# A third buffer for each of the four tags of converted weights, and conversions up to three items ahead

## The chip, the cores and the metric

The kernel runs on one core of a Trainium2 chip. The metric is the device time of one execution in microseconds (us), lower is better; the kernel before is given by the median of three runs. Engines have the profile's names: PE is the matmul engine, PEld its weight loads, DVE the vector engine, ACT the scalar engine, POOL the GpSimd engine, SP the queue that issues most DMAs.

## The reference

One sequence of 512 tokens and width 1024 goes through three layers. The first has three branches (a state-space scan, a delta-rule scan, a gated linear scan), the other two have four (a gated recurrent branch and three kinds of attention). Every layer begins with one wide projection, merges its branches through gates, projects out, and ends with a gated feed-forward block of inner width 2816. Cut to the parts that the change touches:

```python
proj = jnp.einsum('bsd,de->bse', rms_norm(x, norm1_g), w_in)
...
x = x + merged.astype(dt) @ w_out
h2 = rms_norm(x, norm2_g)
ffn = (jax.nn.silu(h2 @ w_ffn_gate) * (h2 @ w_ffn_up)) @ w_ffn_down
return x + ffn
```

## The kernel before, in words

Activations lie feature-major, 128 features by 512 tokens a tile. Each float32 product is made of three float16 products: a weight is scaled by 64 and cut into a high and a low float16 part, as the activations are, and PE adds high x high, high x low and low x high in one PSUM bank (`fm_g`, L1181 to L1183: 128x512 products; `tm`, L1216 to L1218: 128x128 products, operands swapped).

**Weights come in items.** A plain item (a unit) is eight 128x128 blocks, 512 KB of float32. `_emit_unit` (L1057) issues its load on SP into a staging tile (`wst` or `bst`, two buffers each, L1060), converts the high part on ACT (L1070) into `whi` or `bhi`, and the low part on DVE (L1071) into `wlo` or `blo`. The foreground has the `w` tags, the background (the gate projections and the branch outputs) the `b` tags. One plain item of the foreground feeds 24 matmuls of `fm_g`.

**The feed-forward blocks** have a second sort of item. Every third block of the gate and up weights (7 of 22), and the whole down projection, are computed by a seven-product scheme on 256-token halves: `_emit_seventh` (L1092) makes one of the seven weight sums on DVE (L1106, L1110) from staged quarters, converts it on ACT (L1119) and DVE (L1120) into one tile that holds high and low, and puts it into whichever of the four tags is used least (L1115). A seventh with four blocks feeds 12 matmuls of 128x256 (`seventh`, L1424 to L1426). In the gate and up stage, two plain items come first, then a group of seven sevenths, then four plain items, and so on (the list `FOREGROUND`); the down stage is 84 sevenths.

**Who comes when.** `take` (L1136) is called when the matmuls of an item are about to be written. It first gives back the tags of the item before (L1144), then emits loads and conversions of coming items as long as `_room` (L1123) says so, then returns the item. `_room` counts buffers: the background may be one item past the present one (L1130); a plain foreground item needs fewer than three plain items from the present one to it, and fewer than two live buffers in `whi` and in `wlo` (L1133); a seventh needs one tag with fewer than two live buffers, in the feed-forward part only (L1134). A scheduler then orders the instructions of each engine: among those that are ready in its own model of the run, the one written first goes first. On the chip each engine's order is fixed, and an instruction that must wait holds up those behind it. A conversion therefore stands in ACT's and DVE's fixed order among other work: in the gate and up stage among the epilogue of a block (L1440 multiplies PSUM by the row norm on DVE, or on POOL for one of the two halves; L1478 is a tanh on ACT; L1480 on DVE; L1231 and L1235 cut the result into `hh` and `hl`; L1370 makes sums for the seven-product scheme).

After the feed-forward block of one layer the next projection's items follow in the same list, and the first plain ones are converted while the down stage still runs.

Of the kernel before, what the change touches and what calls it, by code (L numbers as in the profile page):

```python
# [11 lines left out]
F16 = mybir.dt.float16  # L12
# [13 lines left out]
PS = 1024.0  # L26
EPS = 1e-6
UB = 8
H = T // 2
FF7 = tuple(range(1, NF, 3))  # L30


def blocks(*ws):
# [6 lines left out]
    b = np.concatenate(seq) if len(seq) > 1 else seq[0]  # L40
    return np.ascontiguousarray(b.reshape(-1, UB, 128, 128).transpose(0, 2, 1, 3))


def paired(a, b):

    k, n = a.shape
    s = np.stack([w.reshape(k // 128, 128, n // 128, 128).transpose(2, 0, 1, 3) for w in (a, b)], axis=1)
    s = s.reshape(-1, UB, 128, 128)
    return np.ascontiguousarray(s.transpose(0, 2, 1, 3))
# [185 lines left out]
class First:  # L235
# [546 lines left out]
    def hgrn(self, yd):  # L782
# [19 lines left out]
        for h in range(4):  # L802
# [23 lines left out]
            nc.gpsimd.tensor_tensor(out=kk, in0=k2[:, 0], in1=k2[:, 1], op=ALU.add)  # L826
            pd = self.b("H")
            for i in range(4):
# [12 lines left out]
            for l in range(7):  # L841
# [6 lines left out]
                if l < 5:  # L848
                    po = self.b("H")
                    for i in range(4):  # L850
# [5 lines left out]
                else:  # L856
                    if l == 5:
                        big = self.b("H")
                    bv = big.rearrange("p (i t) -> p i t", i=4)
# [10 lines left out]
            for d in range(2):  # L870
# [5 lines left out]
                nc.gpsimd.tensor_tensor(out=qp, in0=q, in1=p, op=ALU.mult)  # L876
                pt = self.b("H")
                for i in range(4):
                    nc.tensor.transpose(pt[:, 128 * i:128 * i + 128], kr[:, 128 * i:128 * i + 128], self.ident)
                kt = self.hw()  # L880
                nc.scalar.copy(out=kt, in_=pt)
                pk = self.b("H")
                order = (0, 1, 2) if d == 0 else (3, 2, 1)
# [15 lines left out]
                yield  # L899
            po = self.b("H")  # L900
            for i in range(4):
# [62 lines left out]
class Net(First):  # L964
# [92 lines left out]
    def _emit_unit(self, s, name, u):  # L1057
        nc = self.nc
        tag = "wb"[s]
        st = self.t(self.wst, [128, UB, 128], tag + "st", F32, 2)  # L1060
        nc.sync.dma_start(out=st, in_=self.io[name][u])
        hi = self.t(self.wsp, [128, UB, 128], tag + "hi", F16, 2)
        lo = self.t(self.wsp, [128, UB, 128], tag + "lo", F16, 2)
        if s and self.spare and self.emitted[1] % 2:
            nc.scalar.activation(out=st, in_=st, func=AF.Copy, scale=WS)
            nc.scalar.copy(out=hi, in_=st)
            nc.gpsimd.tensor_tensor(out=lo, in0=st, in1=hi, op=ALU.subtract)
        else:
            for h in (slice(0, UB // 2), slice(UB // 2, UB)) if s and self.spare else (slice(0, UB),):
                nc.scalar.activation(out=hi[:, h], in_=st[:, h], func=AF.Copy, scale=WS)  # L1070
                nc.vector.scalar_tensor_tensor(out=lo[:, h], in0=st[:, h], scalar=WS, in1=hi[:, h], op0=ALU.mult, op1=ALU.subtract)  # L1071
        return hi, lo
# [19 lines left out]
    def _emit_seventh(self, e, name, u, m):  # L1092

        nc = self.nc
        if m == 0:
            st = self._stage(name, u)
            nxt = self.items[0][e + 7] if e + 7 < len(self.items[0]) else ("", 0, None)
            if nxt[2] is not None:
                self._stage(*nxt[:2])
        a11, a21, a22, a12 = self._stage(name, u)  # L1100
        n = a11.shape[1]
        if m in (0, 4, 6):
            src = {0: a11, 4: a22, 6: a12}[m]
        elif m == 5:
            src = self.s2
            nc.vector.tensor_tensor(out=src, in0=a12, in1=src, op=ALU.subtract)  # L1106
        else:
            src = self.t(self.tmp, [128, 4, 128], "bw", F32, 2)[:, 0:n]
            x, y = {1: (a21, a22), 2: (self.s2, a11), 3: (a11, a21)}[m]
            nc.vector.tensor_tensor(out=src, in0=x, in1=y, op=ALU.add if m == 1 else ALU.subtract)  # L1110
            if m < 3:
                self.s2 = src
        if m == 6:
            del self.staged[name, u]
        tag = min(("bhi", "blo", "whi", "wlo"), key=lambda t: self.tags[t])  # L1115
        o = self.t(self.wsp, [128, 2, 4, 128], tag, F16, 2)
        self.tags[tag] += 1
        hi, lo = o[:, 0, 0:n], o[:, 1, 0:n]
        nc.scalar.activation(out=hi, in_=src, func=AF.Copy, scale=WS)  # L1119
        nc.vector.scalar_tensor_tensor(out=lo, in0=src, scalar=WS, in1=hi, op0=ALU.mult, op1=ALU.subtract)  # L1120
        return hi, lo, tag

    def _room(self, s, e, i):  # L1123

        name, _, m = self.items[s][e]
        if e == i:
            return True
        if s:
            at = lambda n: n[-1] if n[:2] == "wi" or n[:3] == "wup" else "f"
            return e < i + 2 and at(name) == at(self.items[s][i][0])  # L1130
        if m is None:
            plain = sum(k is None for _, _, k in self.items[s][i:e + 1])
            return plain < 3 and all(self.tags[t] < 2 for t in ("whi", "wlo"))  # L1133
        return self.opened and min(self.tags.values()) < 2  # L1134

    def take(self, name, u, m=None):  # L1136
        s = int(self.bgmode)
# [1025 lines left out]
```

## Time and profile before

| what | value |
| --- | --- |
| median of three runs | 3617.13 us (3607.03 to 3620.99) |
| the profiled execution | 3613.31 us |
| its span, first to last instruction | 3611.6 us |
| mean granted TensorE clock | 0.976 |
| busy: PE, PEld, DVE, ACT, POOL | 92%, 56%, 76%, 45%, 21% |
| stages of gate and up weights in the span | 1056.7 to 1293.7, 2152.4 to 2396.1, 3251.1 to 3492.6 us |
| stages of down weights in the span | 1293.7 to 1402.7, 2396.1 to 2501.3, 3492.6 to the end |

A matmul's shown length includes its way through the array, and the next one starts before it ends; so the distance between two starts tells what a matmul takes of PE, and an idle time shown on PE is shorter than the time that PE lost. A row of the waits has the waiting engine and line, what it waited for, the total in us, the number of waits and the longest.

### The profile page before, as it was taken

The numbers are of one execution on the slowest core, as the hardware profiler recorded it, in microseconds if no ns is written. First come the engines' busy times: TensorE is split into PE (matmuls) and PEld (weight loads), VectorE is DVE, ScalarE is ACT, GpSimd is POOL, SyncE is SP. The second block draws the span as 40 slices with busy tenths as digits, with TensorE's granted clock in tenths as the row PEclk, the third lists the DMA queues.
The fourth block names the chain that finished last, engine by engine and source line by source line (L and its number), as shares of the span: only waits on it lengthen the run. The fifth ranks groups of instructions, "written<-read, shape, count | busy, mean of one in ns | idle before, by whom it ended". The sixth has DMA issues, their size and how long they took to land. (4 is left out here: it accounts for less than half of the span.)

```text
span 3611.6 us, 60781 instructions
## 1 busy us (share of the span) xinstructions
PE 3338.2 (92%) x23758; PEld 2033.9 (56%) x23758; DVE 2760.1 (76%) x5599; ACT 1608.3 (45%) x3009; POOL 752.6 (21%) x782
## 2 busy tenths in 40 slices
PE   7899999899899999999989999999999989999998
PEld 3565566555455577556545545568655545545567
DVE  6877777587777798788767677788788767777788
ACT  4232333255344344464556543344364455534443
POOL 2222223223332211201221132211201120132211
PEclk9999999899899999999999999999999999999999
DMA  4312213233242234323223353335322323363333
GB/s 141 82 57 59 75 49 91 72 126 114 88 164 94 94 106 146 106 63 96 93 82 109 116 159 96 96 112 159 111 65 80 94 90 100 112 185 110 94 100 94
DMA packets 151156, 368.16 MB, mean 102 GB/s; under 512 B 44098, under 2 KB 47428, under 8 KB 150868
## 3 DMA queue, kind: packets, MB, share of 16 engines
q1 hardware_dynamic: 117492, 336.03, 30.0%
q0 software_dynamic: 7680, 23.00, 1.9%
q10 hardware_dynamic: 25696, 5.25, 0.8%
q8 instruction: 186, 3.05, 0.4%
q14 instruction: 102, 0.84, 0.1%
HBM read 322.72 MB, written 40.04 MB: 100 GB/s over the span
## 5 line engine op out<-in xcount | busy, mean ns | idle before, releaser
L1181 PE MATMUL acc<-xh,whi 128*128 128x512 f16 x1224 | 469.5, 384 | 28.3 <-DVE g L1706 7.5
L1183 PE MATMUL acc<-xh,wlo 128*128 128x512 f16 x1224 | 469.0, 383 | 23.7 <-DVE wlo L1071 23.6
L1182 PE MATMUL acc<-xl,whi 128*128 128x512 f16 x1224 | 468.9, 383 | 0.0
L1070 ACT ACTIVATE whi<-wst 128x1024 f16<-128x1024 f32 x264 | 275.3, 1049 | 310.3 <-PE acc L1182 147.1
L1071 DVE SCALAR_TENSOR_TENSOR wlo<-wst,whi 128x1024 f16<-128x1024 f32 x264 | 353.9, 1341 | 15.9 <-ACT whi L1070 14.3
L1183 PEld LDWEIGHTS <-wlo 128*128 128x128 f16 x1824 | 179.6, 98 | 257.3 <-DVE wlo L1071 51.4
L1182 PEld LDWEIGHTS <-whi 128*128 128x128 f16 x1824 | 179.9, 99 | 226.6 <-issue 41.9
L1181 PEld LDWEIGHTS <-whi 128*128 128x128 f16 x1824 | 180.6, 99 | 210.4 <-issue 12.4
L1183 PE MATMUL bg<-xh,blo 128*128 128x512 f16 x596 | 230.9, 387 | 3.4 <-DVE reset L309 3.2
L1181 PE MATMUL bg<-xh,bhi 128*128 128x512 f16 x596 | 230.9, 387 | 0.4 <-DVE hk L810 0.4
L1182 PE MATMUL bg<-xl,bhi 128*128 128x512 f16 x596 | 230.6, 387 | 0.0
L1440 POOL TENSOR_TENSOR w<-w,w 128x512 f32<-128x512 f32 x66 | 117.5, 1780 | 448.4 <-DVE w L1440 282.1
L1216 PE MATMUL acc<-whi,xh 128*128 128x128 f16 x1152 | 195.1, 219 | 3.1 <-DVE xp L1758 1.3
L1218 PE MATMUL acc<-whi,xl 128*128 128x128 f16 x1152 | 195.0, 219 | 0.0
L1217 PE MATMUL acc<-wlo,xh 128*128 128x128 f16 x1152 | 195.0, 219 | 0.0
L1070 ACT ACTIVATE bhi<-bst 128x1024 f16<-128x1024 f32 (+1 forms) x132 | 121.7, 934 | 129.4 <-PE bg L1182 89.7
L1071 DVE SCALAR_TENSOR_TENSOR blo<-bst,bhi 128x1024 f16<-128x1024 f32 (+1 forms) x132 | 160.8, 1223 | 13.7 <-ACT bhi L1070 12.1
L1183 PE MATMUL bg<-xh,wlo 128*128 128x512 f16 x408 | 157.3, 386 | 9.1 <-DVE wlo L1071 9.1
L1181 PE MATMUL bg<-xh,whi 128*128 128x512 f16 x408 | 157.4, 386 | 3.0 <-ACT whi L1070 1.8
L1182 PEld LDWEIGHTS <-bhi 128*128 128x128 f16 x980 | 97.6, 100 | 109.0 <-issue 20.1
L1183 PEld LDWEIGHTS <-blo 128*128 128x128 f16 x980 | 97.5, 100 | 106.9 <-issue 6.8
L1181 PEld LDWEIGHTS <-bhi 128*128 128x128 f16 x980 | 97.9, 100 | 105.4 <-issue 9.8
(666 smaller groups left out, 9256.9 us busy)
## 6 DMA issues: line engine op xcount, KB each, us to landing
wst<-win SPq DMA_DIRECT2D x92, 512.0 KB, 3.6
bst<-win SPq DMA_DIRECT2D x64, 512.0 KB, 3.7
wst<-wff SPq DMA_DIRECT2D x60, 512.0 KB, 3.5
wst<-w SPq DMA_DIRECT2D x58, 512.0 KB, 3.6
gd<-bw SPq DMA_DIRECT2D x88, 256.0 KB, 2.2
ug<-gd SPq DMA_DIRECT2D x88, 256.0 KB, 2.7
wst<-wf SPq DMA_DIRECT2D x30, 512.0 KB, 3.5
bst<-w SPq DMA_DIRECT2D x20, 512.0 KB, 3.6
```

Of the source, the lines that this page charges most:

```text
L1070: nc.scalar.activation(out=hi[:, h], in_=st[:, h], func=AF.Copy, scale=WS)
L1071: nc.vector.scalar_tensor_tensor(out=lo[:, h], in0=st[:, h], scalar=WS, in1=hi[:, h], op0=ALU.mult, op1=ALU.subtract)
L1181: mm(ps, lhsT=wh, rhs=h[:, k, :], start=(k == 0), stop=False)
L1182: mm(ps, lhsT=wh, rhs=l[:, k, :], start=False, stop=False)
L1183: mm(ps, lhsT=wl, rhs=h[:, k, :], start=False, stop=(k == nk - 1))
L1216: mm(o, lhsT=xh, rhs=wh, start=(k == 0), stop=False)
L1217: mm(o, lhsT=xh, rhs=wl, start=False, stop=False)
L1218: mm(o, lhsT=xl, rhs=wh, start=False, stop=(k == 7))
L1440: tt = lambda eng, o, x, y, op=ALU.add: eng.tensor_tensor(out=o, in0=x, in1=y, op=op)
```

## The change

A constant `WB = 3` takes the place of the number 2 in the buffers of the four tags and in the rule of `_room`. Each tag has three tiles of 2 KB a partition instead of two, 8 KB a partition more in all. A plain foreground item may be emitted with up to three plain items from the present one to it, a background item up to two past the present one, and a seventh while any tag has fewer than three live buffers. The staging tiles stay at two buffers each. No instruction is added or taken out.

```diff
+WB = 3
...
-        hi = self.t(self.wsp, [128, UB, 128], tag + "hi", F16, 2)
-        lo = self.t(self.wsp, [128, UB, 128], tag + "lo", F16, 2)
+        hi = self.t(self.wsp, [128, UB, 128], tag + "hi", F16, WB)
+        lo = self.t(self.wsp, [128, UB, 128], tag + "lo", F16, WB)
...
-        o = self.t(self.wsp, [128, 2, 4, 128], tag, F16, 2)
+        o = self.t(self.wsp, [128, 2, 4, 128], tag, F16, WB)
...
-            return e < i + 2 and at(name) == at(self.items[s][i][0])
+            return e < i + WB and at(name) == at(self.items[s][i][0])
         if m is None:
             plain = sum(k is None for _, _, k in self.items[s][i:e + 1])
-            return plain < 3 and all(self.tags[t] < 2 for t in ("whi", "wlo"))
-        return self.opened and min(self.tags.values()) < 2
+            return plain <= WB and all(self.tags[t] < WB for t in ("whi", "wlo"))
+        return self.opened and min(self.tags.values()) < WB
```

## Rows read from the trace of the kernel before

**Rows 1.** The page's first part: busy time and share of each engine.

```profile
PE 3338.2 (92%) x23758; PEld 2033.9 (56%) x23758; DVE 2760.1 (76%) x5599; ACT 1608.3 (45%) x3009; POOL 752.6 (21%) x782
```

**Rows 2.** Busy time by stretch, the gate and up stages: stretch, us, engines, clock, DMA.

```profile
1056.70:1293.70 237.00, 224.38 (x1327) 128.45 (x1327) 186.20 (x307) 97.84 (x147) 48.11 (x30) 1.00 0.31 100
2152.40:2396.10 243.70, 225.11 (x1326) 127.66 (x1326) 185.90 (x306) 97.79 (x147) 48.09 (x30) 1.00 0.32 95
3251.10:3492.60 241.50, 226.53 (x1327) 128.41 (x1327) 186.17 (x307) 97.83 (x147) 48.08 (x30) 0.99 0.33 100
sum 722.20, PE 676.03 PEld 384.52 DVE 558.26 ACT 293.46 POOL 144.28; mean PE 225.34 PEld 128.18 DVE 186.09 ACT 97.82 POOL 48.09
```

**Rows 3.** PE's timeline: a stall, then 24 products of sevenths, then 48 of plain items.

```profile
2251.47 0.39 PE L1181 MATMUL acc<-xh,whi 128*128 128x512 f16 x1 [0.68 <-ACT whi L1070]
...
2252.91 0.39 PE L1183 MATMUL acc<-xh,wlo 128*128 128x512 f16 x1 [0.84 <-DVE wlo L1071]
...
2264.16 0.27 PE L1424 MATMUL bg<-xsh,blo 128*128 128x256 f16 x1
...
2266.78 0.27 PE L1424 MATMUL acc<-xsh,wlo 128*128 128x256 f16 x1
...
2278.89 0.38 PE L1181 MATMUL bg<-xh,whi 128*128 128x512 f16 x1
...
2289.25 0.38 PE L1181 MATMUL acc<-xh,whi 128*128 128x512 f16 x1
```

**Rows 4.** PE's waits for conversions in the whole span, longest in total first.

```profile
PE acc L1183 <- DVE wlo L1071: 23.6, 26, 1.9
...
PE bg L1183 <- DVE wlo L1071: 9.1, 7, 1.8
...
PE acc L1426 <- DVE whi L1120: 8.2, 12, 1.4
...
PE bg L1426 <- DVE whi L1120: 8.0, 9, 1.1
```

**Rows 5.** Busy time by stretch, the first two down stages, columns as above.

```profile
1293.70:1402.70 109.00, 102.41 (x926) 89.56 (x925) 103.55 (x176) 58.24 (x105) 17.39 (x11) 1.00 0.38 111
2396.10:2501.30 105.20, 102.09 (x925) 89.59 (x924) 98.81 (x176) 54.77 (x100) 12.10 (x12) 1.00 0.49 151
```

**Rows 6.** ACT's timeline around that stall: start, length, work, idle before it.

```profile
2237.82 1.99 ACT L1070 ACTIVATE whi<-wst 128x1024 f16<-128x1024 f32 x2
...
2247.68 0.63 ACT L1231 ACTIVATE hh<-w 128x512 f16<-128x512 f32 x1 [2.17 <-POOL w L1440]
2249.41 1.06 ACT L1231 ACTIVATE hh<-tt 128x1024 f16<-128x1024 f32 x1 [1.10 <-DVE tt L1370]
2250.37 1.04 ACT L1070 ACTIVATE whi<-wst 128x1024 f16<-128x1024 f32 x1
...
2270.92 1.99 ACT L1070 ACTIVATE whi<-wst 128x1024 f16<-128x1024 f32 x2
```

**Rows 7.** The costliest groups and the DMA issues: one conversion, one load.

```profile
L1070 ACT ACTIVATE whi<-wst 128x1024 f16<-128x1024 f32 x264 | 275.3, 1049 | 310.3 <-PE acc L1182 147.1
L1071 DVE SCALAR_TENSOR_TENSOR wlo<-wst,whi 128x1024 f16<-128x1024 f32 x264 | 353.9, 1341 | 15.9 <-ACT whi L1070 14.3
...
wst<-wff SPq DMA_DIRECT2D x60, 512.0 KB, 3.5
```

**Rows 8.** Waits of PE for the attention's own work, and of ACT for buffers.

```profile
PE O L1818 <- ACT pth L1231: 9.1, 9, 1.8
...
PE S L1581 <- ACT w L1572: 8.2, 7, 1.5
...
ACT whi L1070 <- PE acc L1182: 147.1, 53, 12.6
```

**Rows 9.** SP's timeline: loads of the two plain items after that group of sevenths.

```profile
2255.22 7.11 SPq L1061 DMA_DIRECT2D wst<-wff x2
```

**Rows 10.** Busy time by stretch, the second layer up to its feed-forward part, columns as above.

```profile
1402.70:2152.40 749.70, 705.41 (x5282) 404.78 (x5280) 562.28 (x1225) 376.87 (x746) 135.93 (x185) 0.99 0.35 107
```

## The prediction, made before the change was run

> **What bounds the kernel now.** I read the page's first part first: PE is busy for 92% of the span, DVE for 76%, ACT for 45% [rows 1]. PE is the engine to fill, so the question is where it stands still and for whom. The table by stretch answers by stage. In the three stages of gate and up weights DVE is busy 186 of some 240 us and ACT 98, so neither is full; yet PE is idle for 722.2 - 676.0 = 46.2 us in them [rows 2]. The timeline shows how a matmul should go there: 48 products of plain items start from 2278.89 to 2289.25, 0.216 us each, and 24 products of sevenths from 2264.16 to 2266.78, 0.109 us each [rows 3]. A stage has 30 plain items of 24 products and some 607 products of 256 columns or smaller (1327 less 720), so PE needs 720 x 0.216 + 607 x 0.109 = 221.7 us and takes 237.0, 243.7 and 241.5 [rows 2]: 57 us are lost in the three. The list of PE's waits then names the cause: its largest conversion rows, 23.6, 9.1, 8.2 and 8.0 us, hold 54 waits and 48.9 us, none over 1.9 us [rows 4]. They are about as large as the idle time of these stages and of the first two down stages together (46.2, and 6.6 + 3.1 [rows 5]). So conversions arrive late almost only in the feed-forward blocks, and nothing else stops PE in the gate and up stages.
>
> Why are they late, with ACT half idle? The episode at 2250 shows it. Two conversions run at 2237.8; the next stands in ACT's fixed order behind two splits of `hh`, which wait for POOL (2247.68) and for DVE (2249.41), and starts at 2250.37 [rows 6]. PE gets its high part at 2251.47 and its low part at 2252.91, with 0.68 and 0.84 us idle shown [rows 3]. By the rule of `_room` that conversion was for the item that PE was to start at once: after a group of sevenths just one plain item is ready beyond the one at work, because two buffers hold the item in use and the next.
>
> **The change, part by part.** *Buffers and rule for plain items.* I went through `take` by hand for a run of the list. Before, the item after the next is emitted only when PE's present item begins, and in the gate and up stage the lead is one plain item at every plain item. After, it is two; and the first two plain items behind a group of sevenths are emitted before or at that group's first product, where before the first of them came with the group's sixth. One plain item is 24 x 0.216 = 5.2 us of PE. A conversion is 1.05 us of ACT and 1.34 us of DVE [rows 7], unchanged in number and length. The longest shown lateness is 1.9 us [rows 4], under the 5.2 us of lead that is added, so all these stalls can go. The floor of the gain is the idle time shown, 46.2 us; the ceiling is the loss by the distance of starts, 57. An idle time is shown short by the part of a matmul that overlaps the next, 0.38 - 0.22 = 0.16 us [rows 3]; with some 45 of the waits in these stages that adds 7 and makes 53. I keep off 3 us for the norm's small sums, with which each stage begins and which stay (an allowance of mine), and take **50**, between the ends.
>
> *Rule for sevenths.* Twelve tiles instead of eight can be ahead. In the first two down stages PE is idle 6.6 and 3.1 us [rows 5], in the third its idle time is mixed with the kernel's end and I count nothing. DVE is busy 103.6 of 109.0 and 98.8 of 105.2 us there, so a deeper queue cannot feed PE for long; but it is filled in the stage before, where DVE has 50 us free, and four more tiles are a start. Ends 0 and 9.7; I take half, **5**. The Trainium skill (Perfetto Trace Analysis, section Identifying the Most-Contended Engine) holds VectorE's busy share to be a fair measure of how near a stage is to its limit; by that rule the down stages belong to DVE at 94 to 95%, buffers bring nothing there, this term is 0 and the forecast would come out 5 us higher.
>
> *Background, three items in flight instead of two.* Its conversions hardly hold PE today, so nothing is gained directly. Ends: see the next part.
>
> *Order in the other stages.* 264 foreground conversions [rows 7] less 90 of the gate and up stages are 174 that move one item ahead, in each case ACT's, DVE's and SP's instruction. Behind a waiting one on ACT stand the exponentials and splits of the attention, and PE waits for those: 9.1 and 8.2 us today [rows 8]. These could go, or double: ends -17.3 and +17.3. I take 0: the total work is the same, and a conversion still waits for a buffer that is freed at the same product as before. On SP a load moves ahead with it; it is hidden as long as two staging tiles suffice (first rival). The 8 KB a partition cost no time by themselves.
>
> *Sum.* 50 + 5 = 55 us off the profiled execution's 3613.3 (span 3611.6 and 1.7 around it): 3558. That execution is 3.8 us under the median of 3617.1, from which the same sum gives 3562; I say **3560**.
>
> **The rivals.** *Staging takes over.* The loads keep two staging tiles, and a group of sevenths holds one for long, so a conversion may wait for its load instead of its buffer. A plain item through one tile takes 3.5 us of load, 1.05 and 1.34 [rows 7], 5.9 us against 5.2 of PE: 0.7 late, and with two such items for each of 21 groups 30 us of the gain are lost: **3590**. Against it: the load of the item behind the sevenths was issued at 2255.22 [rows 9], so it should have landed near 2258.7, and its conversion ran at 2270.92 [rows 6]. Its tile lay full for 12 us because no buffer was free; staging is ahead of the conversions, not behind.
>
> *Conversions get in the way of the attention: slower.* ACT spends 147.1 us in 53 waits at conversions until PE frees a buffer, 2.8 us each [rows 8], and all that stands behind waits too. If the earlier place puts conversions in front of exponentials, splits and the scans' copies more often, each of the 174 costs PE a little. The gain is used up from 55 / 174 = 0.32 us each; at 0.45 us it is 78 us and the kernel ends at **3638**, slower. For it: PE is idle 44.3 of 749.7 us in the second layer up to its feed-forward part [rows 10], all of it with no conversion to blame, so it hangs on that chain. Against it: today's two largest waits of this kind are 17.3 us in all, and the rival needs more than four times that.
>
> *It does not do what it says.* Sevenths go into any tag, so they may take the third buffer of `whi`, on which plain items hang, and the scheduler may leave the conversions behind the same splits as now. Then the 1 or 2 us of lateness stay, and only the down stages gain: **3611**. Against it: by the walk through `take` plain items have both tags free for a lead of two in every group.
>
> **How the numbers follow.** About half a percent, 18 us, is what a measurement of this kernel can tell from no change: faster is under 3599, slower over 3635. The forecast has 0.67, staging 0.11 (still faster), no effect 0.09 (same), the attention rival 0.13, of which 0.09 slower and 0.04 in between. So faster 0.78, same 0.13, slower 0.09. The range begins where every lost us of the feed-forward blocks and the 17.3 come back, 3613 - 57 - 10 - 17 = 3529, and ends at staging with 17 us lost in the attention, 3607; that leaves out the attention rival and half of the case without effect, 0.17.
>
> **What would show it.** Right: PE's waits for `wlo` at L1183 and for `whi` at L1426 (one line lower in the new file) fall from 49 us to under 10; the three gate and up stages take 224 to 227 us each, with PE's idle time near 2; DVE's busy time there is still 186; the down stages shorten by 1 to 3 us. Staging would show as ACT and DVE waiting for `wst` and PE's waits for conversions of the items behind the sevenths remaining. The attention rival would show as stages from one feed-forward block to the next longer than 749.7, with more waits of PE for exponentials and splits. The forecast is wrong if the gate and up stages stay over 232 us, or if any attention layer moves by more than 10.

## The result, and the profile after

| what | before | after |
| --- | --- | --- |
| median of four runs, us | 3612.26 (3607.03 to 3620.99) | 3578.19 (3561.63 to 3583.99) |
| ratio, 95% interval | | 0.9896 [0.9855, 0.9936] |
| the profiled execution, us (span) | 3613.31 (3611.6) | 3583.99 (3582.3) |
| mean granted clock of it | 0.976 | 0.970 |

The kernel became 1% faster: 34 us by the medians, 29.3 by the two spans. (The ratios in this text are those on record, with their intervals; they differ a little from the ratio of the medians, here 0.9906.) The forecast was 3560; it is missed by 18 us and the result lies in its range. The profiled execution of after is the longest of its four. In the new file the lines of `Gen` touched here stand one lower (L1070 is L1071, L1183 is L1184, L1426 is L1427).

The page's first part, as [rows 1]:

```profile
PE 3345.5 (93%) x23758; PEld 2057.1 (57%) x23758; DVE 2740.0 (76%) x5599; ACT 1607.2 (45%) x3009; POOL 780.4 (22%) x782
```

Busy time by stretch, the three gate and up stages of after, columns and ends as in [rows 2]:

```profile
1073.80:1298.90 225.10, 223.34 (x1326) 130.13 (x1326) 179.39 (x305) 96.28 (x147) 55.03 (x30) 0.99 0.34 111
2161.60:2386.50 224.90, 221.88 (x1326) 129.76 (x1326) 179.13 (x302) 95.57 (x145) 55.04 (x30) 1.00 0.34 102
3238.50:3463.60 225.10, 223.16 (x1326) 130.15 (x1327) 178.90 (x302) 96.11 (x146) 55.04 (x30) 0.99 0.34 104
sum 675.10, PE 668.38 PEld 390.04 DVE 537.42 ACT 287.96 POOL 165.12; mean PE 222.79 PEld 130.01 DVE 179.14 ACT 95.99 POOL 55.04
```

The three stages take 675.1 us where [rows 2] have 722.2, and PE is idle 675.10 - 668.38 = 6.7 us in them where it was 46.2. PE's waits, all the rows for conversions in the span (total us, times, longest), show why:

```profile
PE acc L1427 <- DVE bhi L1121: 4.5, 4, 1.7
...
PE acc L1425 <- ACT bhi L1120: 1.7, 3, 0.9
...
PE acc L1427 <- DVE whi L1121: 1.0, 1, 1.0
...
PE bg L1184 <- DVE blo L1072: 0.7, 1, 0.7
...
PE acc L1427 <- DVE blo L1121: 0.5, 1, 0.5
```

The largest row of [rows 4], 23.6 us of plain products waiting for `wlo`, is gone altogether; 8.4 us are left of all kinds. Now the other stretches: first the two down stages that [rows 5] show, then the three stretches that lead up to a feed-forward block (the second of them is that of [rows 10]), all of after:

```profile
1298.90:1408.20 109.30, 102.72 (x925) 89.92 (x924) 106.07 (x178) 57.86 (x105) 19.09 (x11) 1.00 0.38 110
2386.50:2492.10 105.60, 101.81 (x925) 90.17 (x924) 101.02 (x179) 55.40 (x101) 14.93 (x12) 1.00 0.51 152
...
0.00:1073.80 1073.80, 962.55 (x6455) 584.32 (x6456) 774.59 (x1713) 402.28 (x784) 299.13 (x291) 0.93 0.29 90
1408.20:2161.60 753.40, 704.52 (x5282) 405.84 (x5281) 562.07 (x1225) 377.29 (x748) 133.79 (x185) 0.98 0.35 107
2492.10:3238.50 746.40, 699.78 (x5259) 402.94 (x5257) 554.78 (x1209) 376.75 (x747) 133.81 (x185) 0.99 0.35 108
```

and the same three stretches of before:

```profile
0.00:1056.70 1056.70, 944.21 (x6454) 570.81 (x6455) 777.49 (x1713) 400.06 (x782) 298.13 (x291) 0.95 0.30 92
...
2501.30:3251.10 749.80, 702.18 (x5258) 401.09 (x5257) 556.58 (x1208) 374.92 (x745) 133.40 (x185) 0.98 0.35 107
```

So the 29.3 us of the spans add up like this: gate and up stages -47.1; down stages +0.3, +0.4 and, with the kernel's end, -0.3 (119.0 to 118.7); second layer +3.7, third -3.4; first layer **+17.1**. The gain is there in full, and the first layer gives a third of it back. What it gives back is not a wait: PE is *busy* 962.55 us there instead of 944.21, 18.3 more for the same products, at a granted clock of 0.93 instead of 0.95. That clock is a mean over two levels, 1.2 and 2.4 GHz. One such stretch of after stands out, again by stretch:

```profile
682.00:691.60 9.60, 7.19 (x51) 4.84 (x49) 4.08 (x11) 3.04 (x7) 2.97 (x2) 1.00 0.09 17
691.60:718.90 27.30, 12.96 (x133) 10.21 (x134) 10.06 (x41) 3.38 (x13) 6.54 (x10) 0.50 0.36 119
718.90:728.00 9.10, 8.75 (x43) 4.01 (x41) 7.60 (x23) 1.37 (x2) 0.00 (x0) 1.00 0.26 93
```

For 27.3 us PE has half its speed; in the 9.6 us before it stood still for a quarter of the time, and it goes on standing still for half of it. It shows what low clock looks like, not where the 17 us went: e5 (below), whose whole first layer takes 1050.8 us, has as long a one at much the same work, and before has two there of 13.6 us each.

```profile
668.20:695.50 27.30, 13.65 (x138) 11.04 (x139) 10.12 (x39) 4.21 (x14) 6.43 (x10) 0.50 0.40 132
```

### The profile page after: what moved, and what is told of

It is laid out like the page before. It is cut to its first block, busy times and chain, and to the rows that moved or that the text cites. A ratio compares the mean times of both kernels' runs of the same rounds, so it can differ in the third digit from the quotient of the medians.

```text
span 3582.3 us, 60816 instructions
## 1 busy us (share of the span) xinstructions
PE 3345.5 (93%) x23758; PEld 2057.1 (57%) x23758; DVE 2740.0 (76%) x5599; ACT 1607.2 (45%) x3009; POOL 780.4 (22%) x782
## 4 chain that ended last, share of the span: by engine, by line
PE 36%; DVE 29%; issue 8%; ACT 6%; POOL 5%; DMA 3%; ACTq 0%; POOLq 0%; DVEq 0%; SPq 0%
PE bg L1182 3%; PE bg L1184 3%; PE bg L1183 3%; PE acc L1182 3%; PE acc L1183 3%; PE acc L1184 3%; DVE wlo L1072 3%; POOL w L1441 2%; DVE w L1441 2%; DVE bw L1111 2%; PE acc L1217 1%; PE acc L1218 1%; PE acc L1219 1%; PE acc L1425 1%; DVE hl L1236 1%
## 5 line engine op out<-in xcount | busy, mean ns | idle before, releaser
L1183 PE MATMUL acc<-xl,whi 128*128 128x512 f16 x1224 | 470.8, 385 | 0.0
L1184 PE MATMUL acc<-xh,wlo 128*128 128x512 f16 x1224 | 470.2, 384 | 0.0
L1071 ACT ACTIVATE whi<-wst 128x1024 f16<-128x1024 f32 x264 | 276.7, 1051 | 333.7 <-PE acc L1183 149.6
L1072 DVE SCALAR_TENSOR_TENSOR wlo<-wst,whi 128x1024 f16<-128x1024 f32 x264 | 330.3, 1252 | 29.7 <-ACT whi L1071 28.8
L1183 PEld LDWEIGHTS <-whi 128*128 128x128 f16 x1824 | 180.0, 99 | 241.8 <-issue 56.1
L1184 PEld LDWEIGHTS <-wlo 128*128 128x128 f16 x1824 | 180.0, 99 | 209.0 <-issue 13.7
L1184 PE MATMUL bg<-xh,blo 128*128 128x512 f16 x596 | 230.0, 386 | 3.2 <-DVE reset L310 3.2
L1183 PE MATMUL bg<-xl,bhi 128*128 128x512 f16 x596 | 230.3, 386 | 0.0
L1071 ACT ACTIVATE bhi<-bst 128x1024 f16<-128x1024 f32 (+1 forms) x132 | 121.7, 933 | 112.2 <-PE bg L1183 93.4
L1183 PEld LDWEIGHTS <-bhi 128*128 128x128 f16 x980 | 97.3, 99 | 107.0 <-issue 17.1
L1184 PE MATMUL bg<-xh,wlo 128*128 128x512 f16 x408 | 158.4, 388 | 0.0
L1183 PE MATMUL bg<-xl,whi 128*128 128x512 f16 x408 | 158.3, 388 | 0.0
L1184 PEld LDWEIGHTS <-blo 128*128 128x128 f16 x980 | 97.2, 99 | 102.5 <-issue 7.7
```

Source lines behind the costliest of these rows:

```text
L1183: mm(ps, lhsT=wh, rhs=l[:, k, :], start=False, stop=False)
L1184: mm(ps, lhsT=wl, rhs=h[:, k, :], start=False, stop=(k == nk - 1))
```

## The experiments

Two questions were open. Which part of the change makes the 47 us: the third tile, or the rules that emit items earlier (that write their load and conversions at an earlier place of the program)? And what lengthens the first layer? Four spots of the change can be set one by one: the tiles, and in `_room` the rules for background, plain items and sevenths. In this table "stages" are the three gate and up stages and "first layer" is the time up to the first of them, both from the profiled execution; the clocks are those of all executions of a kernel. Ratios are to the kernel before, measured beside each.

| kernel | stages, us | first layer, us | median, us | ratio | clocks |
| --- | --- | --- | --- | --- | --- |
| before | 237.0, 243.7, 241.5 | 1056.7 | 3612.26 | 1 | .974 to .979 |
| after | 225.1, 224.9, 225.1 | 1073.8 | 3578.19 | 0.9896 [0.9855, 0.9936] | .970 to .977 |
| e3_buffers_only | 226.1, 226.5, 226.1 | 1059.0 | 3576.38 | 0.9918 [0.9903, 0.9934] | .974 to .978 |
| e6_third_w | 227.8, 228.3, 228.3 | 1049.2 | 3567.89 | 0.9894 [0.9877, 0.9911] | .974 to .981 |
| e7_third_b | 237.3, 239.9, 239.9 | 1074.4 | 3623.32 | 1.0045 [1.0032, 1.0057] | .971 to .975 |
| e1_ffn_only | 225.1, 225.9, 226.2 | 1059.8 | 3566.3 | 0.9887 [0.9873, 0.9902] | .974 to .978 |
| e2_outside_only | 226.1, 226.5, 226.1 | 1067.1 | 3579.09 | 0.9922 [0.9903, 0.9942] | .971 to .978 |
| e4_plain_rule | 226.4, 225.8, 228.4 | 1059.8 | 3585.16 | 0.9941 [0.9918, 0.9963] | .971 to .978 |
| e5_background_rule | 226.1, 226.1, 226.8 | 1050.8 | 3566.91 | 0.9894 [0.9881, 0.9908] | .975 to .978 |
| e8_ffn_pool | 225.3, 225.9, 226.2 | 1062.6 | 3589.5 | 0.9956 [0.9943, 0.997] | .972 to .977 |
| e9_changed_again | 225.1, 224.5, 224.4 | 1067.1 | 3575.95 | 0.9888 [0.9874, 0.9902] | .971 to .973 |
| e10_background_old | 225.1, 225.0, 226.5 | 1083.5 | 3580.96 | 0.9905 [0.9881, 0.9929] | .967 to .976 |
| e11_plain_old_outside | 223.1, 224.9, 226.7 | 1066.0 | 3569.3 | 0.9854 [0.9838, 0.9871] | .973 to .978 |
| e12_plain_old_outside_again | 225.3, 226.1, 224.6 | 1051.3 | 3562.07 | 0.9873 [0.9856, 0.9889] | .975 to .978 |

One profile's first layer is a rough measure: e11 and e12 are one kernel, and after and e9 are one, yet their first layers differ by 14.7 and 6.7 us.

**Tiles or rules.** Three tiles, and every rule as before:

```diff
-            return e < i + WB and at(name) == at(self.items[s][i][0])
+            return e < i + 2 and at(name) == at(self.items[s][i][0])
...
-            return plain <= WB and all(self.tags[t] < WB for t in ("whi", "wlo"))
-        return self.opened and min(self.tags.values()) < WB
+            return plain <= 2 and all(self.tags[t] < 2 for t in ("whi", "wlo"))
+        return self.opened and min(self.tags.values()) < 2
```

> Three buffers a tag and all three limits of the rule at two: no conversion is written earlier, but the tile that it writes was freed one item earlier. If the lead in the written order makes the gain (my theory): gate and up stages stay at 237 to 244 us, about 3612. If it is the wait for the tile that made the conversions late: the waits of ACT for PE to free a tile go and the gate and up stages fall to about 225, about 3570.

The stages of e3 by stretch:

```profile
1059.00:1285.10 226.10, 222.39 (x1327) 129.54 (x1327) 183.64 (x303) 96.21 (x146) 48.37 (x30) 1.00 0.32 110
2144.10:2370.60 226.50, 223.84 (x1327) 130.07 (x1327) 183.73 (x302) 96.21 (x146) 48.39 (x30) 0.99 0.32 101
3223.50:3449.60 226.10, 222.23 (x1326) 129.57 (x1326) 183.62 (x302) 96.20 (x146) 48.38 (x30) 1.00 0.33 105
sum 678.70, PE 668.46 PEld 389.18 DVE 550.99 ACT 288.62 POOL 145.14; mean PE 222.82 PEld 129.73 DVE 183.66 ACT 96.21 POOL 48.38
```

722.2 - 678.7 = 43.5 of the 47.1 us come with the tiles alone, while an item is emitted exactly when it was before. The rules are worth the other 3.6, about 1 us a stage. The theory of the written order is refuted by that. Of the other one the times came, but not its sign: ACT's waits for PE to leave a `whi` tile, which were to go, are 147.7 us where they were 147.1 [rows 8]. What the tile changes is seen on ACT, at a place like that of [rows 6]. ACT's timeline of e3 there:

```profile
2225.21 1.06 ACT L1071 ACTIVATE whi<-wst 128x1024 f16<-128x1024 f32 x1
2227.03 1.06 ACT L1071 ACTIVATE whi<-wst 128x1024 f16<-128x1024 f32 x1 [0.76 <-PE bg L1427]
2232.35 0.63 ACT L1479 ACTIVATE w<-w 128x512 f32<-128x512 f32 x1 [4.26 <-DVE w L1441]
2235.14 0.63 ACT L1232 ACTIVATE hh<-w 128x512 f16<-128x512 f32 x1 [2.16 <-POOL w L1441]
2235.68 0.61 ACT L1120 ACTIVATE bhi<-wst 128x512 f16<-128x512 f32 x1
2236.20 0.61 ACT L1120 ACTIVATE bhi<-bst 128x512 f16<-128x512 f32 x1
2236.87 1.06 ACT L1232 ACTIVATE hh<-tt 128x1024 f16<-128x1024 f32 x1
2237.84 1.04 ACT L1071 ACTIVATE whi<-wst 128x1024 f16<-128x1024 f32 x1
```

Behind the `hh` splits a conversion of a plain item stands here as well (2237.84), one of the next sort even between them; but PE's timeline shows no idle time at all from 2225 to 2246. The conversion behind the splits is no longer the one for the item that PE is to start at once. In the list of PE's waits, plain products wait for `wlo` once, for 0.5 us, where [rows 4] have 33 waits and 32.7 us.

**Which tags.** A third tile for `whi` and `wlo` alone, and for `bhi` and `blo` alone, both with the rules of before (the `_room` lines as in e3):

```diff
-        hi = self.t(self.wsp, [128, UB, 128], tag + "hi", F16, WB)
+        hi = self.t(self.wsp, [128, UB, 128], tag + "hi", F16, WB if tag[0] == "w" else 2)
```

with `lo` and the tile of `_emit_seventh` in the same way, and "b" in place of "w" in the other kernel.

> The third buffer for whi and wlo alone, all three limits of the rule at two. If what made conversions late was that a plain item's tile came free too late, the gate and up stages are as short as with all buffers, 212.7 us each (225 to 230 before), and the kernel takes about 3576. If the tiles of the sevenths counted, 218 or more.

> The third buffer for bhi and blo alone, all limits at two. First theory, the plain items' tiles: the gate and up stages stay at 222 to 230 us, about 3605. Rival, the sevenths' tiles: under 218.

PE's waits in e7, the rows for plain products and the largest for sevenths:

```profile
PE acc L1184 <- DVE wlo L1072: 20.4, 25, 1.4
...
PE acc L1427 <- DVE whi L1121: 8.5, 8, 2.4
```

They are those of [rows 4], hardly smaller, and the stages take 717.0 us. With a third `whi` and `wlo` they take 684.4: 37.8 of the 47.1 us. So most of the bound was the pair of `whi` and the pair of `wlo` tiles, the only ones that plain foreground items can take. More `bhi` and `blo` without them made the kernel slower by 0.45% [0.32, 0.57]; its first layer has the low clock again (1074.4 us), and why is not known.

The traces also tell by what way the tile works. In the three stages e7 runs ACT's and DVE's instructions in the order of before, and e6 in that of e3, but for one or two instructions in some stages; and in e3 and e6 the first plain conversion behind each group of sevenths stands ahead of an `hh` split behind which it stood before. ACT's own waits at conversions for PE are small in the stages and hardly changed, 19.3 us in all before and 16.7 in e3. So the third tile acts through the place that the scheduler gives a conversion, with the program's text as it was, more than through a wait on the chip. A late plain conversion had one more effect before, which e3 and e6 no longer have: it kept its staging tile. On DVE, SP and ACT, with ACT's rows for the loads of sevenths:

```profile
2251.64 1.22 DVE L1071 SCALAR_TENSOR_TENSOR wlo<-wst,whi 128x1024 f16<-128x1024 f32 x1
2252.89 0.33 SPq L1087 DMA_DIRECT2D wst<-wff0s  x1
2256.60 0.63 ACT L1119 ACTIVATE bhi<-wst 128x512 f16<-128x512 f32 x1 [3.72 <-DMA wst<-wff0s]
...
ACT bhi L1119 <- DMA wst<-wff0s: 22.6, 7, 3.9
...
ACT bhi L1119 <- DMA wst<-wff1s: 20.4, 7, 5.0
...
ACT bhi L1119 <- DMA wst<-wf1s: 17.3, 7, 3.7
```

The load of the next group's weights starts 0.03 us after DVE has read the plain item's tile, and ACT waits for it, once for each of the 21 groups, 60.3 us in all. In e7 these rows hold 58.6 us, in e3 and e6 0.8 and 0.5. How much of PE's loss came by this way and how much by the conversion itself was not tried apart.

**Rules within the feed-forward blocks, or outside.** First the rules of the change only while a feed-forward block is open, then only outside it, then the rule for plain items everywhere with the two others as before:

```diff
-            return e < i + WB and at(name) == at(self.items[s][i][0])
+            return e < i + 2 and at(name) == at(self.items[s][i][0])
...
-            return plain <= WB and all(self.tags[t] < WB for t in ("whi", "wlo"))
+            lim = WB if self.opened else 2
+            return plain <= lim and all(self.tags[t] < lim for t in ("whi", "wlo"))
```

> Three buffers a tag, but the wider rule for plain foreground items holds only while the feed-forward part is open; elsewhere, and for the background, the rule is the old one (one item past the present one). First theory, the order outside costs: the gate and up stages gain their 51 us as in the changed kernel, the first layer up to its first seventh goes back from 1089 to about 1069 us, and the kernel takes 3612 - 51 = about 3560. Second theory, the 20 us of the first layer are the clock's and fall differently from run to run: no better than the changed kernel, about 3578, with a first layer of 1080 to 1090.

For e2 `lim` is `2 if self.opened else WB`, the last rule is `< 2`, and the background's is that of the change.

> The complement: three buffers a tag, the wider rule for plain foreground items only outside the feed-forward part and for the background; inside it the old limits of two. First theory: the gate and up stages stay at 237 to 244 us with their conversion waits, the first layer takes about 1089 us to its first seventh, and the kernel is slower than before, about 3612 + 20 = 3632. Second theory: as before, about 3612.

For e4 the background's rule is `e < i + 2` and that for sevenths `< 2`; that for plain items is that of the change.

> Three buffers a tag, the wider rule for plain foreground items everywhere, background and sevenths at the old limits. If the plain items' lead makes the gain: the waits for wlo at L1183 (23.6 + 9.1 us) and for whi of plain items (5.5 us) go, those of sevenths for whi at L1426 (16 us) stay, gate and up stages near 227, and the kernel takes about 3575 to 3580 if the first layer keeps its 20 us of loss, 3565 if it was the background's rule that cost them. If the sevenths' lead mattered more: gate and up stages over 232, about 3600.

e1 to e4 were measured together. Against e3, which has the tiles alone, the rules within the feed-forward blocks come with 10 us (3576.38 to 3566.3) and those outside with nothing (3579.09, a ratio within 0.0004 of e3's). Only 1.5 us of the 10 are seen in the profiled stages (677.2 against 678.7), and e6, with every rule as before, has the ratio 0.9894, so their worth is not settled. e4 is the slowest at 3585.16. So the earlier place of items showed no use outside the feed-forward blocks; the first layers of e1 and e2, 1059.8 and 1067.1 us, would speak for a cost there, but that of e4, with the plain rule outside, is 1059.8 too. Neither theory for e2 came, since both left the stages at 237 to 244 us; and the sevenths' waits that were to stay in e4 (16 us for low parts in `whi` at L1426, now L1427) fell to 3.7.

**Is it the background's rule?** After e1, which leaves that rule as before, it was the suspect. So the background's rule alone:

```diff
-            return plain <= WB and all(self.tags[t] < WB for t in ("whi", "wlo"))
-        return self.opened and min(self.tags.values()) < WB
+            return plain <= 2 and all(self.tags[t] < 2 for t in ("whi", "wlo"))
+        return self.opened and min(self.tags.values()) < 2
```

> Three buffers a tag, the wider rule for the background alone; plain foreground items and sevenths at the old limits. It differs from the kernel with buffers alone (3576 us, first layer 1072 us to its first seventh, granted clock 0.974 to 0.978) by that one line. Theory, the background's rule is what costs the first layer its time: first layer of 1080 us or more, a lower granted clock in most runs (0.970 to 0.975) and a slower or equal kernel, 3576 to 3590. Rival, the lower clocks are chance: first layer near 1072, clocks as with buffers alone, about 3576.

It is not: the first layer takes 1050.8 us, less than before, and the clocks are .975 to .978. Then, measured together, the changed kernel once more, the change without the background's rule (`e < i + 2`), and the change with the plain rule of before outside the feed-forward blocks (`lim` as in e1):

> The changed kernel once more, for more executions of it: its first four took 3562 to 3584 us at granted clocks of 0.977 to 0.970, the longest being the profiled one, whose first layer was 20 us longer than before. If the clock makes the spread: again a spread of 15 us or more, with the time falling by some 3 us for every 0.001 of clock, the median between 3565 and 3580, and a profile with a higher clock has a first layer nearer to 1075. If the order of the first layer itself costs the 20 us: 1085 or more at any clock.

> The change with the background's rule put back (one item past the present one); plain items and sevenths as in the change. With the old rule for plain items outside the feed-forward part as well it took 3566 us. If the background's rule and the plain items' rule together made the changed kernel's lower clock: 3563 to 3568, clock 0.975 or more. If the plain items' rule alone did: as the changed kernel, 3578.

> The change with the old rule for plain foreground items outside the feed-forward part; background and sevenths as in the change. Gate and up stages 210 us each as in the change. If the plain items' earlier place in the first layer cost it: first layer 1065 to 1075, and with the gain of the stages the fastest so far, 3555 to 3565. If the background's rule did: 3575 to 3580.

> The kernel of e11_plain_old_outside once more, in a call of its own. In e11 its ratio to the kernel before was 0.9854 [0.9838, 0.9871], where the changed kernel had 0.9888 in the same call; kernels with either rule alone had 0.989 to 0.991. If the earlier place of the plain items outside the feed-forward blocks costs the first layer its clock, the ratio comes out at 0.984 to 0.987 again and the mean granted clock of the executions lies at 0.973 to 0.978. If it was the spread of the granted clock from execution to execution, the ratio comes out at 0.988 to 0.990, as that of the changed kernel. In both the gate and up stages take 209.6 to 211.3 us from the first product of a seventh to the down stage, since the rules within the feed-forward blocks are those of the change.

Taking the background's rule away helps nothing (0.9905 against 0.9888). Taking the plain rule away outside does in this comparison: 0.9854 [0.9838, 0.9871], the interval of e9 begins at 0.9874 (by the medians it is 6.7 us). The same kernel again gave 0.9873 [0.9856, 0.9889], between the two expectations and with an interval that meets e9's; and e1, which differs from it in the background's rule alone, has 0.9887. So the size is not settled, and the gain itself rests on one comparison. The first layer of four kernels by stretch, in the order after (shown above), e10, e12, e5, tells what the difference is made of:

```profile
0.00:1083.50 1083.50, 968.05 (x6454) 585.91 (x6455) 772.59 (x1713) 401.99 (x784) 298.80 (x291) 0.93 0.29 89
```

```profile
0.00:1051.30 1051.30, 944.09 (x6455) 570.78 (x6456) 774.56 (x1713) 402.05 (x784) 297.25 (x291) 0.95 0.30 92
```

```profile
0.00:1050.80 1050.80, 943.44 (x6454) 571.37 (x6455) 773.81 (x1714) 401.83 (x784) 299.56 (x291) 0.95 0.29 92
```

Between e10 and e12 the layer differs by 32.2 us and PE's busy time by 24.0, with the same work in it on every engine: most of the difference is the clock. Over all executions, the five kernels that have the plain rule of the change outside (after, e2, e4, e9, e10) were granted 0.973 or less in 16 of 26; the seven with a third `whi` and `wlo` and the old rule there (e1, e3, e5, e6, e11, e12 and e8, which follows) in 3 of 31, two of these in e8. Among kernels measured together it is 5 of 12 against 0 of 8 (e2 and e4, e1 and e3) and 8 of 10 against 1 of 5 (e9 and e10, e11). That the rule goes with a lower clock is shown. How the order of conversions takes PE below its clock is not; and e7, with the old rule, was granted 0.973 or less in 3 of 5, so it is not the only way there.

**The down stages.** If DVE bounds them, work taken off DVE should shorten them. With the rules of e1, two of the three sums of down weights that DVE makes at L1111 were given to POOL, those of `m` 1 and 3:

```diff
-            nc.vector.tensor_tensor(out=src, in0=x, in1=y, op=ALU.add if m == 1 else ALU.subtract)
+            (nc.gpsimd if m != 2 and name[:2] == "wd" else nc.vector).tensor_tensor(out=src, in0=x, in1=y, op=ALU.add if m == 1 else ALU.subtract)
```

> The kernel with the wider rule in the feed-forward part alone (3566 us), and in the down stages three of the four weight sums of a group of sevenths made on POOL instead of DVE. The down stages did not shorten with the change; DVE was busy 106 of 109 us in the first. If DVE bounds them, taking 12 x 3 x 0.68 = 24 us off it a stage lets PE go: from 109, 105 and 103 us between their first and last products to 101 to 104 each, about 3566 - 8 = 3558. If the chain of one group bounds them (load, sum, ACT, DVE), a sum of 1.8 us on POOL in place of 0.68 makes them longer: 110 or more, 3570 or slower.

The expectation speaks of three of four sums and reckons with three; the edit moves two of the four. The down stages became longer, and the kernel slower than e1, 3589.5 us (0.9956) against 3566.3. The first down stage of e8 by stretch, and three of the groups of DVE and POOL in it (shape, count, busy us, mean ns, idle before):

```profile
1287.90:1404.50 116.60, 104.36 (x926) 89.53 (x925) 109.91 (x157) 58.28 (x105) 51.49 (x33) 1.00 0.34 102
```

```profile
L1107 DVE TENSOR_TENSOR bw<-bst,bw 128x512 f32<-128x512 f32 x8 | 11.5, 1443 | 0.1
L1121 DVE SCALAR_TENSOR_TENSOR bhi<-bw,bhi 128x512 f16<-128x512 f32 x9 | 7.7, 862 | 0.6 <-ACT bhi L1120 0.3
...
L1111 POOL TENSOR_TENSOR bw<-wst,bst 128x512 f32<-128x512 f32 x8 | 12.5, 1566 | 8.7 <-DVE whi L1121 3.7 <-DVE bhi L1121 2.2 <-DMA bst<-wd 1.6
```

The same stage and groups of e1, where DVE does it all:

```profile
1284.90:1394.10 109.20, 102.64 (x925) 89.88 (x924) 106.00 (x178) 57.83 (x105) 19.09 (x11) 1.00 0.37 110
```

```profile
L1107 DVE TENSOR_TENSOR bw<-bst,bw 128x512 f32<-128x512 f32 x8 | 8.7, 1085 | 0.0
...
L1121 DVE SCALAR_TENSOR_TENSOR bhi<-bw,bhi 128x512 f16<-128x512 f32 x9 | 6.8, 767 | 0.2 <-ACT bhi L1120 0.2
...
L1111 DVE TENSOR_TENSOR bw<-wst,bst 128x512 f32<-128x512 f32 x8 | 5.5, 685 | 0.1
```

DVE has 21 instructions less and is busy 3.9 us longer: its sums at L1107, beside POOL's work, took 1443 ns in the mean instead of 1085, and the moved sum itself 1566 on POOL instead of 685. The stage became 7.4 us longer, more than DVE's busy time did. The numbers are those of the second theory (110 us or more, 3570 or slower), in which the chain of one group bounds the stage; but since DVE did not become lighter, the first theory was not put to the test. What bounds the down stages stays open; the experiment shows that POOL is no way to a lighter DVE here. The Trainium skill (SBUF — State Buffer, section SBUF: two separate sides) says that an instruction of VectorE with two inputs in SBUF and one of GpSimd take turns at a shared pair of ports; the lengthened sums have two inputs in SBUF. e8's trace agrees: of the eight sums at L1107 the two that began just before an instruction of POOL took 0.68 us, the six that began while one was at work 1.64 to 1.75.

## Why the prediction was right, and where it was wrong

- **Size of the main gain: right.** 50 us were predicted for the three gate and up stages and 47.1 measured; 224 to 227 us each were named, and they take 224.9 to 225.1. The rows that were to fall from 49 us to under 10 hold 1.0; with conversions of every kind it is 63.8 us before and 8.4 after. PE's idle time is 2.2 us a stage, near the 2 named. The size was read from PE's idle time, which any cure of the late conversions gives back, so it came out although the cause was named wrongly; in that it was lucky.
- **Cause of it: the failed step.** The prediction said that a conversion is late "by the rule of `_room`", since the lead is one plain item at every plain item, and paid the gain to a lead of two. With the rule as it was, e3 has 43.5 of the 47.1 us. The third tile does it, above all that of `whi` and `wlo` (e6, 37.8 us): a conversion needs a tile that PE has left, with two tiles that is the tile of the item just finished, with three the one before that. The lead of which the prediction spoke was that of the emission; what counted was from when on a tile is free for the conversion. That ACT's and DVE's order changes with this tile, and not with the third `bhi` and `blo`, is seen in e6 and e7; that the order makes the whole gain is argued, since no run changed it by itself.
- **Rule for sevenths: wrong, 5 us predicted, none measured.** The first two down stages went from 109.0 and 105.2 to 109.3 and 105.6, and DVE is busy for 97 and 96% of them (106.07 of 109.30, 101.02 of 105.60). Four tiles of a start, filled in the stage before, were of no use there. That it is DVE's own work which fills the stage is likely by these shares, but not shown: e8 failed to lighten DVE. The 0 that the prediction cites beside its 5, by the Trainium skill's rule (Perfetto Trace Analysis, section Identifying the Most-Contended Engine), was the better of the two; the trace agrees with it.
- **DVE's busy time "still 186": wrong.** It fell to 179, with 2 to 5 instructions fewer in the stretch and the low part of a conversion at a mean of 1252 ns instead of 1341 [rows 7]; POOL's 30 sums rose from 48.1 to 55.0. Neither is on PE's path, and in e3 they are 184 and 48.4.
- **Order in the other stages: the term that was mis-sized.** It was put at 0 between -17.3 and +17.3, and argued from the attention's waits for exponentials and splits. These did not move: the second and third layer changed by +3.7 and -3.4, under the 10 named, and PE's waits for `pth` are 7.7 us where they were 9.1 [rows 8]. The +17.1 came from the first layer, at which the prediction had not looked, and not as a wait but as a lower clock. The profiled execution took 25.7 us more than the sum's 3558: 17.4 are this term, 5.4 the sevenths, 2.9 the main gain. Part of the 17.4 is that execution's low clock; the one of after with 0.977 took 3561.63.
- **Staging takes over: did not happen.** ACT's waits for loads of gate and up weights are 9.1 us in after, 5.1 of them for plain items. The argument that the tile lay full held for plain items. For sevenths "ahead of the conversions, not behind" was wrong of the kernel before: there ACT waited 60.3 us for their loads (the rows behind e7), which the prediction did not see and the third tile took away.
- **Conversions get in the way of the attention: did not happen**, see above; ACT's waits for `whi` tiles are 149.6 us where they were 147.1 [rows 8].
- **It does not do what it says: did not happen**, but it holds of e7, with third tiles of the wrong tags.

Of the kernels tried, the change with the plain rule of before outside the feed-forward blocks has the lowest ratios (e11 and e12, 0.9854 and 0.9873). It is ahead of the change where both were measured together.

## What to carry to other kernels

When a rule in the program and a number of buffers both limit how far work runs ahead, find out which one binds by changing one at a time: here, in the profiled stages, the tile was worth 43.5 us and the rule 3.6. Give more lead only in the stage whose waits ask for it: elsewhere it brought nothing that showed, and went with a lower clock. Before a deeper buffer is priced, look at whether the engine that fills it has time left in that stage: in the down stages, with DVE busy for 94 to 97%, four more tiles brought nothing.

## What the runs showed of the hardware that was not expected

- The granted clock moved with the order of conversions while the work stayed the same: 0.974 to 0.979 in before, 0.967 to 0.978 in the kernels with the plain rule outside, 0.972 to 0.981 in those with third `whi` and `wlo` tiles and the old rule there. Among the four executions of after, 0.970 went with 3583.99 us and 0.977 with 3561.63: 3.2 us for each 0.001.
- The clock shows as busy time of PE, not as idle time: over the first layer PE's busy time ran from 943.4 us (e5) to 968.1 (e10) for the same 6454 matmuls in the records. A comparison of idle times alone misses it.
- A sum of 128x512 float32 that took DVE 685 ns took POOL 1566, and DVE's other sums in that stage went from a mean of 1085 to 1443.
